# DeltaNet in a two-layer hybrid decoder: stores moved to ScalarE's and GpSimd's queues, one exponential for each head's decays, beta and the decays ahead of the first convolution

## The chip, the cores and the metric

The kernel runs on one core of a Trainium2 chip. The core has TensorE for matmuls (PE in the profile, its weight loads PEld), VectorE (DVE) and ScalarE (ACT) for elementwise work, GpSimd (POOL), and SyncE (SP), which here only issues DMAs. ScalarE and GpSimd can issue DMAs too; a DMA stands in the issuing engine's instruction queue like any other instruction. The metric is the device time of the whole program in microseconds, the median of several executions. Lower is better.

## The reference

A trunk of two layers over 16 meta tokens and 512 tokens, width 1024: retention, SwiGLU FFN, gated DeltaNet, SwiGLU FFN, and a last RMSNorm. The change lies in DeltaNet alone:

```python
qkv = jax.nn.silu(causal_conv(qkv, conv_w))            # four taps
q = l2norm(q) * (DN_DK ** -0.5); k = l2norm(k)          # 8 heads, dk 128, dv 256
beta = jax.nn.sigmoid(beta_in) * vmask
g = -jnp.exp(a_log) * jax.nn.softplus(a_in + dt_bias) * vmask
# per chunk of a head:
gam = jnp.cumsum(gc, axis=-2)
decay = jnp.exp(jnp.where(incl, gam - jnp.swapaxes(gam, -1, -2), -jnp.inf))
a_mat = jnp.where(strict, bc * kk * decay, 0.0)
sol = triangular_solve(eye + a_mat, [vc * bc, kc * bc * jnp.exp(gam)])
v_new = u - w @ state
qk = (qc @ kc.T) * decay
o = (qc * jnp.exp(gam)) @ state + qk @ v_new
state = state * jnp.exp(g_last) + (kc * jnp.exp(g_last - gam)).T @ v_new
```

Then each head's output is normed, multiplied by the Silu of its gate and projected.

## The kernel before

**Tiling.** Tokens are 16 meta tokens (NM) and 512 others in four chunks of 128; most tiles hold 128 channels by 528 tokens. Every fp32 weight tile and activation is split into a rounded part and a rest: ScalarE writes the rounded part (`whi`, L179 or L460), VectorE the rest (`wlo`, L180 or L461), and TensorE makes three matmuls for one (L470). Raw weight tiles `wraw` are fetched by SyncE (L173) into four buffers.

**Order of the work.** The program text is written out by a planner. A gemm calls `tick` once per slice of 128 contracted rows (6 matmuls of 264 columns); other work is written as Python generators that wait in a heap with a due time in ticks (`spawn`), and each `yield n` puts the next part n ticks later. The framework under it then orders each engine's instructions by their readiness in its own model, with the written order as priority, so that a late-written instruction whose inputs are ready can come before an earlier one that waits. On the chip each engine then works through its own queue in that order.

**DeltaNet** (`deltanet`, from L1764):

1. The first two q and k tiles are multiplied (`gemm_pair`) while the row norm `rb` is finished. Then `dn_gates` is spawned with no delay, so its first part is written after the first slice of the next gemm.
2. `dn_keys` runs for eight heads: a gemm for k and one for q, each followed by `conv_evac` (PSUM times `rb` into `pad` on VectorE, L1202; first tap on ScalarE, L1205; three taps on VectorE, L1207; Silu on ScalarE, L1210), a store of the tile to DRAM (`d_kq`, L1378), and its split `z` (L460, L461). Two `pad` buffers alternate. q tiles get their sums of squares in `dn_norms` (L1400). 13 ticks later comes `dn_attention`: 128x128 products, the vectors `ssk`, `cc`, `kws`, `irk`, the product of scores, `cc` and decays into `vs` (L1446), and a store of it to DRAM (`d_mp`, L1454).
3. `dn_gates` makes what the heads' decays need, in parts: first part (to L1246) 32 matmuls for beta and the decay inputs (L1235) into one large PSUM tile, one evacuation (L1243); 3 ticks later the second part (to L1289), transposes by small matmuls (L1252), sigmoid and softplus by exponentials (L1263, L1269) and a series on VectorE, up to `g` (L1281); 6 ticks later cumulative sums (L1292), their store to DRAM (`d_g`, L1305) and its broadcast load per head (`rows_in`, L1311) into `dec`; 3 ticks later the meta decays `decm0`. Then for each pair of heads GpSimd adds a triangular mask of 1e30 to `dec` (L1356), and ScalarE takes four exponentials per head, one per chunk, with scale -1 and the chunk's sums as per-row bias (L1363). `dec` uses three buffers for even pairs (tag `zh`) and three for odd ones (`zl`); the gates' own work takes one of each first. The second head of pairs 2 and 3 therefore waits until a head of pair 0 or 1 has been used. If a head's attention comes due before its decays, it drives the generator forward (L1407).
4. After the last head: `dn_inverse` loads the 32x32 diagonal blocks of `d_mp` (L1491, SyncE and ScalarE), solves them by substitution on VectorE (L1466 to L1478), stores them (L1496, L1497), and does the same for the meta tokens by way of `d_m0` and `d_m1` (L1498 to L1507). Beside it run value gemms (`dn_values`) and gate gemms (`dn_silu_gate`, with the store `d_sg`, L1608).
5. Four pairs of heads go through `dn_merge` (blocks up to 128x128; it loads `u` from `d_x`, L1515, and transposes it, L1516), `dn_scan` and `dn_gated`, between further value, gate and output gemms.

**Who issues what.** Before the change SyncE issues nearly all DMAs of this layer: weight loads, `d_kq`, `d_mp`, `d_g`, `d_m0`, `d_m1`, `d_sg` and the loads of `u`. Its queue is in order: a store that waits for its data holds up the loads behind it.

Of the kernel before, what the change touches and what calls it, by code (L numbers as in the profile page):

```python
# [10 lines left out]
AF = mybir.ActivationFunctionType  # L11
ALU = mybir.AluOpType
# [4 lines left out]
KT = D // P  # L17
NM = 16
NT = 512
T = NM + NT  # L20
HH = T // 2
# [29 lines left out]
PAIRS_APART = 14  # L51
MASKED = 4
VALUES = 6
GATE_STEPS = (3, 6, 3)
# [5 lines left out]
class Hybrid:  # L60
# [1130 lines left out]
    def conv_silu(self, w, x, rb, mt):  # L1191

        nc = self.nc
        p = self.psum_g()
        self.gemm(p, w, x, range(KT))
        return self.conv_evac(p, rb, mt)

    def conv_evac(self, p, rb, mt):
        nc = self.nc
        self.pads.reverse()  # L1200
        pad = self.pads[0]
        nc.vector.tensor_tensor(self.halves(pad[:, 3 : 3 + T]), p[:, :, :HH], self.halves(rb), op=ALU.mult)  # L1202
        acc = self.t(self.tp, [P, T], "ra", bufs=4)
# [9 lines left out]
    def dn_gates(self, sp, x, rb):  # L1213


        nc, a = self.nc, self.a
# [13 lines left out]
        nc.vector.tensor_copy(pick[32:48], self.ident[32:48, 32:48])  # L1230
        p = self.psum_g()
        for kt in range(KT):
            for i in range(2):
                for half in range(2):
                    nc.tensor.matmul(  # L1235
                        p[:48, half, :HH],
                        wst[:, kt, :],
# [4 lines left out]
        ba = self.t(self.tp, [P, T], "ra", bufs=4)[:48]  # L1242
        nc.vector.tensor_tensor(self.halves(ba), p[:48, :, :HH], self.halves(rb[:48, :]), op=ALU.mult)  # L1243
        bm = self.t(self.tp, [P, 96], "am", bufs=1)
# [101 lines left out]
        for pair in range(DH // 2):  # L1346
# [13 lines left out]
            for hd in hds:  # L1360
                for c in range(4):
                    o, de = (c + 1) * DH + hd, self.dec[hd][:, c]
                    nc.scalar.activation(de, de, AF.Exp, scale=-1.0, bias=sums[:, o : o + 1])  # L1363
            self.decays = 2 * pair + 2

    def dn_keys(self, pool, hd, x, rb, first, gt):

        nc, a = self.nc, self.a
        for s, base in ((1, 0), (0, 8)):
            if first is None:  # L1370
                w = self.load_w(a["w_dqk"][hd, 1 - s])
                p = self.psum_g()
                self.gemm(p, w, x, range(KT))
            else:
                p = first.pop(0)
            t_ = self.conv_evac(p, rb, base + hd)
            real = t_[:, NM:].rearrange("p (c i) -> p c i", c=4)
            nc.sync.dma_start(self.d_kq[:, hd, :, s, :], real)  # L1378
            if s == 1:
# [24 lines left out]
    def dn_attention(self, pool, hd, zh, zl, gt):  # L1404
# [40 lines left out]
        for c in range(4):  # L1445
# [7 lines left out]
            )  # L1453
        nc.sync.dma_start(self.d_mp[:, 4 * hd : 4 * hd + 4], mp)  # L1454
        nc.vector.scalar_tensor_tensor(
# [25 lines left out]
    def dn_inverse(self, sp):  # L1481
# [11 lines left out]
        for b in range(4):  # L1493
# [3 lines left out]
            eng.dma_start(self.d_mp[bs, :, 0, bs].rearrange("j q i -> q j i"), d[bs])  # L1497
        nc.sync.dma_start(self.d_m0, self.decm0)  # L1498
        nc.sync.dma_start(dm, self.d_m0.rearrange("j h i -> h j i"))
        yield from self.substitute(dm, tmp, NM)  # L1500
        nc.sync.dma_start(self.d_m1.rearrange("j h i -> h j i"), dm)
        um = self.t(sp, [96, DH, NM], "rr")
        nc.gpsimd.memset(um, 0.0)
        for b in range(3):
            (nc.sync, nc.scalar)[b % 2].dma_start(um[32 * b : 32 * b + NM], self.d_m1)
        nc.scalar.copy(self.um, um)
        nc.vector.tensor_tensor(self.um[64:96], um[64:96], self.um[64:96].bitcast(F32), op=ALU.subtract)  # L1507

    def dn_merge(self, hd, z, sp):
# [4 lines left out]
        ut = self.t(sp, [P, 4, 32], "wl")  # L1514
        nc.sync.dma_start(uc, self.d_x[:, 4 * hd : 4 * hd + 4])  # L1515
        nc.vector.transpose(ut.rearrange("p a b -> p (a b)"), uc.rearrange("p a b -> p (a b)"))  # L1516
# [81 lines left out]
    def dn_silu_gate(self, hd, x, rb):  # L1598
# [8 lines left out]
        nc.scalar.activation(sg, sg, AF.Silu)  # L1607
        nc.sync.dma_start(self.d_sg[:, hd], sg)  # L1608

# [154 lines left out]
    def deltanet(self, st, ctx, nxt):  # L1764
# [44 lines left out]
        rb = st["rb"]  # L1809
        gt = self.spawn(self.dn_gates(sp, x, rb))  # L1810
        for hd in range(DH):
# [276 lines left out]
```

## Time and profile before

| what | us |
|---|---|
| median of 3 executions | 1672.09 |
| lowest, highest of them | 1669.11, 1672.17 |
| the profiled execution's own time | 1669.76 |
| its span, first to last instruction | 1668.0 |
| its mean granted TensorE clock | 0.996 |
| the window from 795 to 942 (keys and attention of DeltaNet) | 147, TensorE busy 140.44 |
| 942 to 1000 (inverse) | 58, TensorE busy 56.56 |
| 1000 to 1325 (merges, scans, outputs) | 325, TensorE busy 320.02 |

Line numbers (L470) are those of the kernel before. A matmul's end is modelled and matmuls overlap, so busy TensorE isn't TensorE at its best rate: it helps to count matmuls per window and to look at the granted clock, too. A row of waits has the waiting instruction, who ended the wait, the total, the number of times and the longest. A group's row has line, engine, operation, output and inputs, shapes, count, then busy time and mean duration, then idle time of the engine before them. DMA issues of an engine aren't counted as busy; in timelines they stand with a q behind the engine's name, and a number ahead of a bracketed arrow is idle time and who ended it.

### The profile page before, as it was taken

Reading aid. Unit: us, or ns where it says so; the run is one execution under the profiler, and the core shown is the slowest. Engines: PE = TensorE matmul, PEld = TensorE weight load, DVE = VectorE, ACT = ScalarE, POOL = GpSimd, SP = SyncE. Lnnn points to the kernel's source line nnn. Section 1 sums busy time; section 2 is a strip of 40 time slices with the busy share of each in tenths; the row PEclk is TensorE's granted clock in tenths of the full one; section 3 lists DMA queues with packets and bytes.
Section 4 is the critical chain, followed back from the end, with each engine's and each line's share of the span. In section 5 each row is a group of like instructions: output and inputs, shape, how many; then the busy total and the mean of one; then the engine's idle time right before and its main releaser. Section 6 shows DMA issues by size and latency. Waiting matters only on the chain.

```text
span 1668.0 us, 30777 instructions
## 1 busy us (share of the span) xinstructions
PE 1643.1 (99%) x12415; PEld 1550.9 (93%) x12415; DVE 1297.6 (78%) x2121; ACT 886.1 (53%) x1536; POOL 99.7 (6%) x139
## 2 busy tenths in 40 slices
PE   9999999999999999999989999999999999999998
PEld 9999999999999999999989988888877889999896
DVE  7886877798698887784689888796876798888672
ACT  5445555555345545543595427776663455555542
POOL 1000000000000000000030000010100000000010
PEclk9999999999999999999999999999999999999999
DMA  6564746565323332453354554432323223333451
GB/s 211 175 165 119 219 111 198 176 210 167 113 89 102 102 102 82 122 155 101 102 158 159 140 143 139 156 104 89 107 75 114 90 89 113 102 107 110 114 163 52
DMA packets 91888, 214.54 MB, mean 129 GB/s; under 512 B 20394, under 2 KB 42146, under 8 KB 90466
## 3 DMA queue, kind: packets, MB, share of 16 engines
q1 hardware_dynamic: 80066, 194.21, 35.3%
q0 software_dynamic: 4688, 16.53, 5.7%
q10 hardware_dynamic: 6992, 1.85, 0.5%
q8 instruction: 97, 1.59, 0.4%
q14 instruction: 45, 0.37, 0.1%
HBM read 190.30 MB, written 22.25 MB: 127 GB/s over the span
## 4 chain that ended last, share of the span: by engine, by line
PE 86%; DVE 9%; ACT 3%; issue 2%; POOL 1%; POOLq 0%; ACTq 0%; DVEq 0%
PE g L470 66%; PE m L470 14%; DVE wlo L461 1%; ACT whi L460 1%; DVE wsum L220 1%; DVE ra L1207 1%; PE m L573 0%; DVE flt L461 0%; POOL ss L1686 0%; PE m L559 0%; PE m L704 0%; DVE wlo L180 0%; DVE wraw L312 0%; DVE flb L461 0%; PE m L143 0%
## 5 line engine op out<-in xcount | busy, mean ns | idle before, releaser
L460 ACT CAST whi<-wraw 128x1024 fp32r<-128x1024 f32 x171 | 179.2, 1051 | 192.5 <-PE g L470 69.4
L470 PE MATMUL g<-fht,whi 128*128 128x264 f32 (+1 forms) x976 | 277.4, 284 | 0.8 <-DVE h L338 0.7
L470 PE MATMUL g<-fht,wlo 128*128 128x264 f32 (+1 forms) x976 | 276.1, 283 | 0.8 <-DVE wlo L461 0.8
L470 PE MATMUL g<-flt,whi 128*128 128x264 f32 (+1 forms) x976 | 275.9, 283 | 0.0
L470 PE MATMUL g<-xlo,whi 128*128 128x264 f32 (+1 forms) x1088 | 260.9, 306 | 0.0
L470 PE MATMUL g<-xhi,whi 128*128 128x264 f32 (+1 forms) x1024 | 251.8, 310 | 4.6 <-ACT whi L179 4.0
L470 PE MATMUL g<-xhi,wlo 128*128 128x264 f32 (+1 forms) x1024 | 251.2, 308 | 2.3 <-DVE wlo L180 2.3
L461 DVE TENSOR_TENSOR wlo<-wraw,whi 128x1024 fp32r<-128x1024 f32 x171 | 210.5, 1234 | 46.5 <-ACT whi L460 46.2
L179 ACT CAST whi<-wraw 128x1024 fp32r<-128x1024 f32 (+3 forms) x117 | 118.1, 1011 | 138.5 <-PE g L470 107.1
L470 PEld LDWEIGHTS g<-fht,whi 128*128 128x128 f32 x976 | 183.8, 188 | 1.3 <-ACT ra L540 0.9
L470 PEld LDWEIGHTS g<-fht,wlo 128*128 128x128 f32 x976 | 183.6, 188 | 1.1 <-DVE wlo L461 1.0
L470 PEld LDWEIGHTS g<-flt,whi 128*128 128x128 f32 x976 | 183.7, 188 | 0.5
L470 PEld LDWEIGHTS g<-xlo,whi 128*128 128x128 f32 x1088 | 176.7, 189 | 7.0 <-DVE xlo L529 0.2
L470 PEld LDWEIGHTS g<-xhi,whi 128*128 128x128 f32 x1024 | 167.8, 190 | 12.4 <-ACT whi L179 4.2
L470 PEld LDWEIGHTS g<-xhi,wlo 128*128 128x128 f32 x1024 | 167.3, 189 | 10.1 <-DVE wlo L180 3.3
L180 DVE TENSOR_TENSOR wlo<-wraw,whi 128x1024 fp32r<-128x1024 f32 (+3 forms) x117 | 138.0, 1180 | 40.5 <-ACT whi L179 39.5
L470 PE MATMUL g<-fhb,whi 128*128 128x264 f32 (+1 forms) x480 | 137.4, 286 | 0.0
L470 PE MATMUL g<-fhb,wlo 128*128 128x264 f32 (+1 forms) x480 | 136.1, 284 | 1.0 <-DVE wlo L461 0.8
L470 PE MATMUL g<-flb,whi 128*128 128x264 f32 (+1 forms) x480 | 135.7, 283 | 0.0
L461 DVE TENSOR_TENSOR wlo<-wsum,whi 128x1024 fp32r<-128x1024 f32 x54 | 66.1, 1225 | 44.5 <-ACT whi L460 44.5
L470 PEld LDWEIGHTS g<-fhb,wlo 128*128 128x128 f32 x480 | 90.3, 188 | 1.8 <-DVE wlo L461 1.8
L470 PEld LDWEIGHTS g<-flb,whi 128*128 128x128 f32 x480 | 90.3, 188 | 0.5
(562 smaller groups left out, 3804.4 us busy)
## 6 DMA issues: line engine op xcount, KB each, us to landing
wraw<-in_w_gu_dram SPq DMA_DIRECT2D x66, 512.0 KB, 3.4
wraw<-in_w_ret_dram SPq DMA_DIRECT2D x56, 512.0 KB, 3.7
sraw<-in_w_gu_dram SPq DMA_DIRECT2D x22, 512.0 KB, 4.1
wraw<-in_w_ret_dram POOLq DMA_DIRECT2D x18, 512.0 KB, 5.6
wraw<-in_w_dqk_dram SPq DMA_DIRECT2D x16, 512.0 KB, 3.4
wraw<-in_w_dv_dram SPq DMA_DIRECT2D x16, 512.0 KB, 3.3
wraw<-in_w_dg_dram SPq DMA_DIRECT2D x16, 512.0 KB, 3.9
wraw<-in_w_do_dram SPq DMA_DIRECT2D x16, 512.0 KB, 3.4
```

The lines of the kernel that those rows point to most:

```text
L179: nc.scalar.copy(hi[:, c], raw[:, c])
L180: nc.vector.tensor_tensor(lo[:, c], raw[:, c], hi[:, c].bitcast(F32), op=ALU.subtract)
L220: nc.vector.scalar_tensor_tensor(dst[:, k, :], hh[:, kb + k, cs], g[:, kb + k : kb + k + 1], rb[:, cs], op0=ALU.mult, op1=ALU.mult)
L460: self.nc.scalar.copy(hi, src)
L461: self.nc.vector.tensor_tensor(lo, src, hi.bitcast(F32), op=ALU.subtract)
L470: mm(o, l, r[which], start=first and n == 0, stop=last and n == 2, **kw)
L1207: nc.vector.scalar_tensor_tensor(acc, pad[:, i : i + T], cw[:, mt, i : i + 1], acc, op0=ALU.mult, op1=ALU.add)
```

## The change

Four things are changed, all in DeltaNet.

- **Queues.** The stores `d_kq` (16) and `d_sg` (8) are issued by ScalarE, the stores `d_mp` (8), `d_m0`, `d_m1`, the load back of `d_m0`, the three loads of `d_m1` and the eight loads of `u` by GpSimd.
- **Exponentials.** Per head, four Identity activations (one per chunk, 128x128, the same scale and bias as before) are followed, 2 ticks later (RAISED), by one Exp over 128x512 in place.
- **Gates first.** Both first convolutions are evacuated to `pad` at once; then the first two parts of `dn_gates` are written with no tick between them, and only then the first head's taps. The third part is due 6 ticks later as before.
- **PSUM.** The first part's matmuls go to two small PSUM tiles, evacuated one by one, and no longer to one large one.

```diff
@@ -1193,13 +1194,16 @@
-        return self.conv_evac(p, rb, mt)
+        return self.conv_taps(self.conv_pad(p, rb), mt)
 
-    def conv_evac(self, p, rb, mt):
-        nc = self.nc
+    def conv_pad(self, p, rb):
         self.pads.reverse()
         pad = self.pads[0]
-        nc.vector.tensor_tensor(self.halves(pad[:, 3 : 3 + T]), p[:, :, :HH], self.halves(rb), op=ALU.mult)
+        self.nc.vector.tensor_tensor(self.halves(pad[:, 3 : 3 + T]), p[:, :, :HH], self.halves(rb), op=ALU.mult)
+        return pad
+
+    def conv_taps(self, pad, mt):
+        nc = self.nc
         acc = self.t(self.tp, [P, T], "ra", bufs=4)
...
@@ -1228,19 +1232,21 @@
-        p = self.psum_g()
+        p = [self.psum_m()[:48, :HH] for half in range(2)]
...
-                        p[:48, half, :HH],
+                        p[half],
...
-        nc.vector.tensor_tensor(self.halves(ba), p[:48, :, :HH], self.halves(rb[:48, :]), op=ALU.mult)
+        for half in range(2):
+            hs = slice(half * HH, half * HH + HH)
+            nc.vector.tensor_tensor(ba[:, hs], p[half], rb[:48, hs], op=ALU.mult)
@@ -1360,7 +1366,10 @@
-                    nc.scalar.activation(de, de, AF.Exp, scale=-1.0, bias=sums[:, o : o + 1])
+                    nc.scalar.activation(de, de, AF.Identity, scale=-1.0, bias=sums[:, o : o + 1])
+            yield RAISED
+            for hd in hds:
+                nc.scalar.activation(self.dec[hd], self.dec[hd], AF.Exp)
@@ -1369,13 +1378,11 @@
-                p = self.psum_g()
-                self.gemm(p, w, x, range(KT))
+                t_ = self.conv_silu(w, x, rb, base + hd)
             else:
-                p = first.pop(0)
-            t_ = self.conv_evac(p, rb, base + hd)
+                t_ = self.conv_taps(first.pop(0), base + hd)
...
-            nc.sync.dma_start(self.d_kq[:, hd, :, s, :], real)
+            nc.scalar.dma_start(self.d_kq[:, hd, :, s, :], real)
...
-        nc.sync.dma_start(self.d_mp[:, 4 * hd : 4 * hd + 4], mp)
+        nc.gpsimd.dma_start(self.d_mp[:, 4 * hd : 4 * hd + 4], mp)
...
-        nc.sync.dma_start(self.d_m0, self.decm0)
-        nc.sync.dma_start(dm, self.d_m0.rearrange("j h i -> h j i"))
+        nc.gpsimd.dma_start(self.d_m0, self.decm0)
+        nc.gpsimd.dma_start(dm, self.d_m0.rearrange("j h i -> h j i"))
...
-        nc.sync.dma_start(self.d_m1.rearrange("j h i -> h j i"), dm)
+        nc.gpsimd.dma_start(self.d_m1.rearrange("j h i -> h j i"), dm)
...
-            (nc.sync, nc.scalar)[b % 2].dma_start(um[32 * b : 32 * b + NM], self.d_m1)
+            nc.gpsimd.dma_start(um[32 * b : 32 * b + NM], self.d_m1)
...
-        nc.sync.dma_start(uc, self.d_x[:, 4 * hd : 4 * hd + 4])
+        nc.gpsimd.dma_start(uc, self.d_x[:, 4 * hd : 4 * hd + 4])
...
-        nc.sync.dma_start(self.d_sg[:, hd], sg)
+        nc.scalar.dma_start(self.d_sg[:, hd], sg)
...
@@ -1807,7 +1814,11 @@
         rb = st["rb"]
-        gt = self.spawn(self.dn_gates(sp, x, rb))
+        first = [self.conv_pad(p, rb) for p in first]
+        gt = self.dn_gates(sp, x, rb)
+        for _ in range(2):
+            next(gt)
+        self.spawn(gt, GATE_STEPS[1])
         for hd in range(DH):
```

More of the change, by code (lines that the diff above doesn't have):

```diff
@@ L52 @@
 MASKED = 4
+RAISED = 2
 VALUES = 6
```

## The prediction

> **What bounds the kernel now.** I read the page first: busy time, share of the span and instructions of each engine.
>
> ```profile
> PE 1643.1 (99%) x12415; PEld 1550.9 (93%) x12415; DVE 1297.6 (78%) x2121; ACT 886.1 (53%) x1536; POOL 99.7 (6%) x139
> ```
>
> TensorE sets the time, and the change takes no matmul away. It can win only where TensorE waits or is slowed, or lose by a new wait. So the second view is the table of windows over the key stage of DeltaNet (columns: window; its length; busy us of TensorE, its weight loads, VectorE, ScalarE and GpSimd with instruction counts; granted TensorE clock; DMA share; GB/s).
>
> ```profile
> 826.00:851.00 25.00, 25.00 (x219) 24.84 (x219) 21.72 (x54) 20.74 (x52) 13.22 (x10) 1.00 0.58 159
> 851.00:861.90 10.90, 9.04 (x71) 8.43 (x70) 9.27 (x26) 10.20 (x23) 0.00 (x0) 1.00 0.43 146
> 861.90:866.20 4.30, 0.31 (x4) 0.07 (x2) 4.04 (x16) 4.27 (x8) 1.16 (x1) 0.97 0.26 84
> 866.20:872.60 6.40, 5.85 (x25) 5.54 (x26) 5.51 (x8) 6.34 (x14) 0.00 (x0) 0.50 0.75 172
> 872.60:897.60 25.00, 25.00 (x209) 25.00 (x209) 20.63 (x59) 15.96 (x32) 3.63 (x3) 1.00 0.51 174
> ```
>
> The last row is the healthy rate: 209 matmuls in 25 us, 0.1196 us each. By it the 71 matmuls of the second row need 8.5 us of its 10.9 (2.4 lost), the 4 of the third 0.5 of 4.3 (3.8 lost), the 25 of the fourth 3.0 of 6.4 (3.4 lost, nearly all to the clock at 0.50). That is **9.6 us between 851 and 872.6**. The first row, 219 matmuls in 25 us, has the healthy rate, so nothing is to be won in the 25 us ahead of the hole.
>
> Who ended TensorE's waits there (table of waits, TensorE alone, 850 to 870; us in total, times, longest):
>
> ```profile
> PE g L470 <- ACT whi L179: 4.0, 1, 4.0
> PE m L1424 <- DVE km L616: 1.0, 1, 1.0
> ```
>
> The long one waits for ScalarE's rounding of a weight tile. The chain of waits of the same stretch (start, us, what) tells why ScalarE was late:
>
> ```profile
> 854.40 1.28 ACT L1363
> 855.70 0.44 ACT zh L1363 x2
> ...
> 856.41 1.28 ACT L1210
> ...
> 859.50 1.28 ACT L1363
> 860.80 1.21 ACT zh L1363 x4
> ...
> 862.10 1.28 ACT L1210
> ```
>
> The 1.28 us entries are loads of the activation table, to Exp for the decays (L1363) and back to Silu (L1210). From 854 to 863 ScalarE spends 4 x 1.28 + 0.44 + 1.21 = 6.8 us on six exponentials and the loads around them. The code writes eight in a row, but here two and four of them stand apart with Silus between: the order on an engine goes by readiness, and late-written exponentials fill gaps.
>
> **The change part by part.** *One exponential per head.* ScalarE's groups from 801 to 872.5 (busy us, mean ns | idle before):
>
> ```profile
> L1210 ACT ACT_TABLE_LOAD x8 | 10.3, 1283 | 0.1
> L179 ACT CAST whi<-wraw 128x1024 fp32r<-128x1024 f32 x9 | 9.3, 1047 | 0.0
> L1205 ACT ACTIVATE ra<-pad,convw 128x528 f32<-128x528 f32 x9 | 6.6, 729 | 2.6 <-DVE pad L1202 2.6
> L1363 ACT ACT_TABLE_LOAD x5 | 6.4, 1283 | 0.1
> L1210 ACT ACTIVATE ra<-ra 128x528 f32<-128x528 f32 x9 | 5.8, 645 | 5.1 <-DVE ra L1207 5.0
> ```
>
> The 32 exponentials become 32 Identities of the same shape and operands (0.3 us each, by the chain's 1.21 for four, so no change), and 8 exponentials of 128x512 come on top. None of that width is in this trace; the Silu of 128x528 takes 0.645, so I take 0.63, or 8 x 0.63 = 5.0 us. Identity isn't in the trace either: nothing more if it needs no table, up to 2 x 1.28 us for each time it would break into the Silus. I take nothing, since the nine Copies (L1205) stand among Silus and exponentials without one load of their own. What it removes: a head's decays can break into the Silus once, not two or three times. Of the five loads for L1363 here, each with a way back, I expect two or three to go, 2 to 3 x 2.57 = 5 to 8 us. ScalarE's sum over the stage is then about even (bounds: 5 more if no load goes, 3 less); what matters is where the loads stand.
>
> The Trainium skill, "ScalarE: Activation LUTs", section "What ACT_TABLE_LOAD costs", has about 1283 ns for a load plus a drain of about 1380 ns, 2.66 us a switch. In the chain the load at 854.40 ends at 855.68 and the exponential starts at 855.70, so no drain shows here. By the page the pairs removed would be worth 10 to 16 us; the measurement decides.
>
> *Beta and the decays first.* Their present times (timelines of the engines: start, us, engine, line, operation):
>
> ```profile
> 806.07 0.41 PE L1235 MATMUL g<-xhi,zl 128*48 128x264 f32 x2
> ...
> 822.74 0.20 DVE L1281 SCALAR_TENSOR_TENSOR g__01460_9425<-zh,alog__01448_9330 128x40 f32<-128x40 f32 x1
> ...
> 833.20 3.53 POOL L1356 TENSOR_TENSOR zh<-zh,kh 128x512 f32<-128x512 f32 x2 [5.96 <-DMA zh<-d_g]
> ```
>
> From L1235 to g takes 16.7 us, because taps of convolutions stand between and three ticks separate the first two steps. Without these the chain is 4 us of matmuls, some 2.5 us of evacuation, transposes and copies, and about 19 small VectorE steps of the 0.2 us that the L1281 row shows: near 11 us, so g comes some 5 us earlier (bounds: 0, if readiness had already decided it, and 7). The store of the sums, its broadcast loads and the additions (L1356) follow. Two evacuations of half width for one cost VectorE perhaps 0.2 us; two small PSUM banks for a big one leave a gemm bank free. The first head's taps come some 4 us later; nothing waits for them before that head's attention, thirteen ticks on. Heads 0 to 4 and 6 can then have their exponentials before 851. Heads 5 and 7 can't: their buffers come free only when heads 0 and 2 have read theirs.
>
> *Stores from ScalarE.* L1378 and L1608 issue behind the Silu that makes their data. SyncE's waits from 801 to 872.5, the store's own row, and ScalarE's timeline at the inverse:
>
> ```profile
> SPq L1378 <- ACT ra L1210: 20.5, 6, 5.2
> ```
> ```profile
> L1378 SPq DMA_DIRECT2D d_kq<-ra x16: 359/371/918, 809.1 to 923.1; - x16
> ```
> ```profile
> 941.21 1.08 ACTq L1491 DMA_DIRECT2D z<-d_mp  x2
> 942.33 0.47 ACT L1579 ACTIVATE v<-m,irk 96x256 fp32r<-96x256 f32 x1 [2.00 <-issue]
> ```
>
> SyncE stood 20.5 us behind Silus, but no wait of TensorE above names a DMA, so freeing it gains 0 here (at most part of the 0.55 us that is left of the hole after the long wait). On ScalarE a store costs its issue, 0.37 us by its row on SyncE; the last row shows ScalarE idle for 2.00 us while a DMA at its head waits. Queued behind each store are the cast of the same Silu's output (L460) and the next rounding (L179), for which TensorE waits. Bounds: 0 where ScalarE has slack, 16 x 0.37 = 5.9 us over the stage; three fall into the critical stretch, 1.1 us. The eight gate stores fall beside the scans: 0 to 3.0 us, I take 0.5.
>
> *Stores and loads from GpSimd.* The list of DMA issues (KB each, median us to landing), then VectorE's timeline where the inverse starts, SyncE's u loads and the transpose behind them:
>
> ```profile
> wraw<-in_w_ret_dram POOLq DMA_DIRECT2D x18, 512.0 KB, 5.6
> ...
> d_mp<-vs SPq DMA_DIRECT2D x8, 512.0 KB, 2.7
> ...
> fnw<-in_fnw_dram POOLq DMA_DIRECT2D x1, 512.0 KB, 4.0
> ```
> ```profile
> 947.06 0.69 DVE L1466 TENSOR_SCALAR z<-z 128x1024 f32<-128x1024 f32 x1 [0.52 <-DMA z<-d_mp]
> ```
> ```profile
> 1055.06 1.40 SPq L1515 DMA_DIRECT2D wh<-d_x  x2
> ```
> ```profile
> 1057.57 0.30 DVE L1516 STREAM_TRANSPOSE wl<-wh 128x128 f32<-128x128 f32 x1
> ```
>
> 512 KB from GpSimd's queue land in 4.0 to 5.6 us against 2.7, so 1.3 to 2.9 later. Of the d_mp stores only the last has a reader near: the inverse at 947.06 waits for it. TensorE has value and gate gemms to do there, so of 1.3 to 2.9 us I count 0.5 on the end (bounds 0 and 2.9). The u load that ends its transpose's wait in the last two rows has no slack for 1.3 us: I count 0.2 (bounds 0 and 2.9). The small meta-token loads run beside the big steps: 0, and as a rival below.
>
> **Sum.** In the critical stretch ScalarE loses 6.8 us of loads and exponentials and gains 1.1 of stores; if head 5's decays still fall here, also 2.57 + 0.63 + 4 x 0.3 = 4.4. Relief is 1.3 or 5.7 us; I take the middle, 3.5, against 3.8 lost in the gap. The 1.0 us wait for km lies in a window whose clock stayed at 1.00, so a rest of that size keeps the clock. Then 3.8 falls to 0.6 and 3.4 to 0.2; the 2.4 ahead falls to 1.4, as small gate steps leave VectorE's queue earlier. 9.6 becomes 2.2, **7.4 gained**. Back go 0.5 + 0.5 + 0.2 = 1.2. What is late next is VectorE, 21 to 22 us busy in 25. The profiled execution took 1669.76: 1669.76 - 6.2 = 1663.6. It lies 2.3 below the median of 1672.09 but inside the three runs' spread (1669.11 to 1672.17), so I say **1664**; this case alone spans 1659 to 1668.
>
> **The rivals.**
> *All of it goes* (0.08): heads 5 and 7 miss the stretch too, 9.6 gained, 1660, by the spread of the runs 1657 to 1662.
> *It doesn't do what it says* (0.16): each head's one exponential still parks between Silus, and relief is 1.3 us or nothing. For it: ScalarE's sum is even. Against it: g is earlier. 1669.
> *GpSimd's queue* (0.10): the last d_mp store, then the store and the loads of the meta inverse, each 1.3 to 2.9 later, one behind the other: 4 to 8 us at the scans' start, of which TensorE's gemms hide some. The 6.2 are given back: 1669. The Trainium skill, "SBUF — State Buffer" (the box "The 'DVE blocks DMA' trap"), has GpSimd unable to write descriptors while VectorE holds the shared port; the trace shows the later landing, not its cause.
> *Slower* (0.16): ScalarE from 845 to 866. No pair of loads goes, and four wide exponentials (2.5) and six stores (2.2) come in: the gap grows by 4.7, all of it at TensorE, since ScalarE is busy for 4.27 of the gap's 4.30. 1669.76 + 4.7 = 1674.5, from the median 1676.8: 1676. It decides once stores and wide exponentials outweigh the loads saved, that is with fewer than two pairs saved.
>
> **How the numbers follow.** The forecast has 0.50. About 0.2% (3.3 us) is what a measurement of this kernel can tell from no change. Faster: 0.50 + 0.08 = 0.58. Same: 0.16 + 0.10 = 0.26. Slower: 0.16. The range takes in the forecast, the cases at 1669 and the edges of the two others: 1657 to 1676.
>
> **What would show it.** Right: fewer than five table loads for the decays by 872, g near 817, the first additions near 828, no wait for whi over 1 us near 862, a clock of 1.00 from 850 to 875. Wrong: a wait of TensorE of 3 us or more between 845 and 880 behind loads and stores on ScalarE, or new idle time of TensorE ahead of the first merges near 1000.

## The result and the profile after

| what | before | after |
|---|---|---|
| median (lowest to highest) of five executions, us | 1670.46 (1669.11 to 1672.17) | 1686.95 (1683.33 to 1688.53) |
| the profiled execution's own time, us | 1669.76 | 1688.53 |
| its span, us, and granted clock | 1668.0, 0.996 | 1686.7, 0.990 |

The ratio is 1.0094, 95% interval 1.0080 to 1.0108: the change makes the kernel **15.7 us slower** (0.0094 x 1670.5). The prediction said 1664 and a range up to 1676; both the sign and the range were wrong.

The page after, busy time by engine:

```profile
PE 1650.7 (98%) x12415; PEld 1556.8 (92%) x12415; DVE 1295.3 (77%) x2122; ACT 885.0 (52%) x1540; POOL 112.8 (7%) x161
```

TensorE makes the same 12415 matmuls as before, so the time was lost in waits between them or at a lower clock. To place it I take, from all matmul rows of a trace, the distance from one start to the next less the pitch of that width in undisturbed stretches (0.122 us for 264 columns, 0.233 for 512, 0.117 for 256, for others columns / 2.4 ns + 6 ns). This "lost time" counts waits and a halved clock together. It is 79.0 us before and 96.6 after, 17.6 more: 3.4 more from 800 to 950, **10.9 more from 950 to 1025**, 3.2 more from 1025 to 1400, 0.1 elsewhere. Only such differences are used below. The level depends on the pitch taken for the narrowest matmuls (98.1 and 115.8 us, if the formula is used down to 1 column); the differences by stretch move by 0.1 us at most. Outside the three stretches, where the program wasn't changed, the profiled executions of the runs below differ from before by up to 2.6 us, so a difference of 1 or 2 us between two single traces says little.

The changed kernel's waits of TensorE alone, 800 to 1025 (us in total, times, longest), answer to the waits shown of before:

```profile
PE g L471 <- ACT whi L180: 13.2, 3, 8.6
PE m L1431 <- DVE km L617: 1.3, 1, 1.3
```

Before, the longest wait near 1000 was one of 1.4 us, in this row of the same table:

```profile
PE g L470 <- DVE wlo L180: 2.3, 3, 1.4
```

So one wait of 8.6 us is new (the expectations below call it 8.8, the length of its whole window). Windows of the changed kernel, the key stage first, then the place of that wait (columns as in the prediction; the DMA share is the time that DMA packets took, as a share of 16 engines' time):

```profile
826.00:851.00 25.00, 20.27 (x164) 19.60 (x163) 19.85 (x56) 19.34 (x47) 13.17 (x11) 1.00 0.55 169
851.00:876.00 25.00, 22.42 (x151) 21.81 (x151) 17.78 (x40) 21.14 (x48) 1.19 (x1) 0.80 0.40 124
...
1000.30:1009.10 8.80, 0.22 (x2) 0.01 (x1) 1.71 (x6) 2.19 (x4) 2.27 (x5) 0.78 0.64 200
1009.10:1014.00 4.90, 4.84 (x19) 4.30 (x19) 4.18 (x5) 2.76 (x6) 0.00 (x0) 0.50 0.64 209
```

From 826 to 851, where TensorE ran without a gap before, it is now idle for almost 5 us: the old hole moved 14 us ahead. From 1000.3 to 1009.1 almost nothing runs on TensorE, and for the next 9.8 us, until 1019.0, its granted clock is 0.50 (the last row shows the first half of that). ScalarE's and then GpSimd's timeline show what the long wait hangs on:

```profile
993.58 0.90 ACTq L1504 DMA_DIRECT2D d_mp<-z  x1
1006.91 0.30 ACT L1513 CAST um<-rr 96x128 fp32r<-96x128 f32 x1 [20.14 <-DMA z<-d_mp]
1007.12 1.05 ACT L1614 ACTIVATE sg<-sg 128x1024 f32<-128x1024 f32 x1
1008.07 1.03 ACT L180 CAST whi<-wraw 128x1024 fp32r<-128x1024 f32 x1
```
```profile
994.39 0.62 POOL L1508 DMA_DIRECT2D d_m<-z  x1 [47.40 <-DVE z L1485]
999.93 1.63 POOL L1512 DMA_DIRECT2D rr<-d_m  x3 [4.92 <-issue]
1001.69 1.14 POOL L1522 DMA_DIRECT2D wh<-d_x  x2
```

ScalarE does nothing for 12 us but wait to round `um`, the meta tokens' inverse, which comes in by three loads of 8 KB from GpSimd's queue (`rr`, landed at 1003.7, 1006.0 and 1006.8; the bracket names another DMA, one of several that are waited for, but the last to land ahead of 1006.91 is `rr`). Behind it in ScalarE's queue stand a Silu and the rounding of the weight tile that TensorE needs. The kernel before had the same step elsewhere (its ScalarE timeline):

```profile
997.68 0.32 ACTq L1505 DMA_DIRECT2D rr<-d_m  x1
998.16 1.99 ACT L179 CAST whi<-wraw 128x1024 fp32r<-128x1024 f32 x2
1000.71 1.23 ACT L1521 COPY oq<-wl 32x128 f32<-32x128 f32 x4 [0.56 <-DVE wl L1516]
1002.37 0.27 ACT L1534 COPY rh<-m 128x128 f32<-128x128 f32 x1 [0.44 <-PE m L1526]
1004.42 0.30 ACT L1506 CAST um<-rr 96x128 fp32r<-96x128 f32 x1 [1.78 <-DMA rr<-d_m]
```

There two weight roundings stand ahead of `um`.

### The profile page after: what moved, and what is told of

It is laid out like the page before. It is cut to its first block, busy times and chain, and to the rows that moved or that the text cites. A ratio compares the mean times of both kernels' runs of the same rounds, so it can differ in the third digit from the quotient of the medians.

```text
span 1686.7 us, 30754 instructions
## 1 busy us (share of the span) xinstructions
PE 1650.7 (98%) x12415; PEld 1556.8 (92%) x12415; DVE 1295.3 (77%) x2122; ACT 885.0 (52%) x1540; POOL 112.8 (7%) x161
## 4 chain that ended last, share of the span: by engine, by line
PE 77%; DVE 12%; ACT 3%; issue 3%; DMA 3%; POOL 1%; ACTq 0%; SPq 0%; POOLq 0%; DVEq 0%
PE g L471 59%; PE m L471 14%; DVE wlo L462 2%; DVE ra L1211 1%; DVE wlo L181 1%; ACT whi L461 1%; DVE z L1485 1%; DVE z L1479 1%; DVE wsum L221 1%; DVE wraw L313 1%; DVE vs L1453 0%; PE m L574 0%; DVE flt L462 0%; POOL ss L1693 0%; PE m L560 0%
```

## The experiments

All ratios are to the kernel before, run on the same chip beside each experiment. Lost time is in us, by the same count as above, for the stretches 800 to 950, 950 to 1025 and 1025 to 1400 of the profiled execution.

| run | median us | ratio (95%) | lost 800 | 950 | 1025 |
|---|---|---|---|---|---|
| before | 1670.5 | 1 | 16.4 | 2.6 | 31.2 |
| after | 1687.0 | 1.0094 (1.0080 to 1.0108) | 19.8 | 13.5 | 34.4 |
| 1 after, meta chain back | 1681.6 | 1.0057 (1.0040 to 1.0074) | 18.5 | 6.6 | 34.5 |
| 2 after, um's steps on GpSimd | 1691.1 | 1.0112 (1.0096 to 1.0127) | 20.0 | 13.6 | 36.5 |
| 3 before + meta chain | 1674.6 | 1.0020 (1.0010 to 1.0031) | 15.7 | 7.0 | 30.8 |
| 4 after, all of GpSimd's back | 1674.1 | 1.0013 (1.0003 to 1.0024) | 17.6 | 2.5 | 32.4 |
| 5 before + one Exp | 1668.0 | 0.9981 (0.9968 to 0.9993) | 14.0 | 2.7 | 31.8 |
| 6 before + gates first | 1670.7 | 0.9991 (0.9979 to 1.0002) | 15.4 | 2.8 | 31.6 |
| 7 before + ScalarE's stores | 1673.2 | 1.0004 (0.9992 to 1.0015) | 16.3 | 2.7 | 32.3 |
| 8 after, only d_mp on GpSimd | 1676.1 | 1.0020 (1.0008 to 1.0033) | 18.8 | 2.4 | 32.4 |
| 9 before + one Exp + gates first | 1672.4 | 1.0010 (0.9999 to 1.0022) | 17.7 | 5.5 | 30.3 |
| 10 run 9, sums subtracted by GpSimd | 1672.4 | 1.0007 (0.9997 to 1.0017) | 16.7 | 2.6 | 30.7 |
| 11 run 5, sums subtracted by GpSimd | 1670.3 | 0.9998 (0.9989 to 1.0008) | 16.3 | 2.6 | 30.0 |
| 12 after, loads of d_m1 back | 1680.0 | 1.0054 (1.0035 to 1.0073) | 18.9 | 4.4 | 33.6 |
| 13 before + u loads | 1673.3 | 1.0010 (0.9998 to 1.0022) | 15.8 | 2.9 | 34.6 |
| 14 before + all queue changes | 1685.4 | 1.0075 (1.0048 to 1.0102) | 16.4 | 11.6 | 34.5 |
| 15 before + meta chain + u | 1677.0 | 1.0047 (1.0032 to 1.0062) | 15.4 | 6.8 | 33.5 |
| 16 before + meta chain + d_mp | 1675.5 | 1.0027 (1.0016 to 1.0039) | 16.6 | 6.8 | 31.0 |
| 17 before + meta chain + d_sg | 1681.3 | 1.0061 (1.0044 to 1.0078) | 15.6 | 10.7 | 33.3 |
| 18 after, d_sg back on SyncE | 1680.8 | 1.0055 (1.0040 to 1.0070) | 17.6 | 7.7 | 33.7 |

"Before + meta chain" means that part of the change alone. The framework orders each engine's instructions anew for every program, so an edit of one queue can shift others; where an order matters below, it is that of the timeline or of the program. Waits of TensorE are those of its matmuls in the table of waits; the expectations have some of them 0.1 to 0.2 us longer. Differences in us are ratio differences times 1670.5.

**First: which of GpSimd's DMAs (runs 1 to 4).** Run 1, and run 4 with `d_mp` and `uc` in the same way:

```diff
-        nc.gpsimd.dma_start(self.d_m0, self.decm0)
-        nc.gpsimd.dma_start(dm, self.d_m0.rearrange("j h i -> h j i"))
+        nc.sync.dma_start(self.d_m0, self.decm0)
+        nc.sync.dma_start(dm, self.d_m0.rearrange("j h i -> h j i"))
...
-        nc.gpsimd.dma_start(self.d_m1.rearrange("j h i -> h j i"), dm)
+        nc.sync.dma_start(self.d_m1.rearrange("j h i -> h j i"), dm)
...
-            nc.gpsimd.dma_start(um[32 * b : 32 * b + NM], self.d_m1)
+            (nc.sync, nc.scalar)[b % 2].dma_start(um[32 * b : 32 * b + NM], self.d_m1)
```

> The changed kernel with only the meta-token chain (d_m0, its load back, d_m1, its three loads) back on SyncE and ScalarE. Theory Q (ScalarE's queue): in the changed kernel ScalarE's rounding of the meta block (um) was ordered ahead of a Silu and of the rounding of the next weight tile, and stands 20.1 us for the loads from GpSimd's queue; TensorE waits 8.8 us behind it and runs the next 5 us at clock 0.50, 10.7 us by the windows from 975 to 1025. With a load on ScalarE again the rounding is ordered behind two weight tiles: no wait of TensorE over 2 us from 990 to 1020, and 1686.95 - 10.7 = 1676 (1674 to 1679). Theory L (late d_mp store or late u loads hold the inverse; the meta chain only shows it): these two stay on GpSimd, so the wait stays at 5 us or more and the time at 1683 or above.

> The changed kernel with every DMA that went to GpSimd back on SyncE and ScalarE (d_mp, meta chain, u); ScalarE's stores, the one exponential and the order of the gates stay. Theory Q: the meta chain is nearly all of what GpSimd's queue costs, so this equals the run with the meta chain back, 1676, within 2 us. If the d_mp stores and u loads cost by themselves (my prediction had 0.7 for them, bounds 0 and 5.8), it is lower by that. What is left above 1670.5 then belongs to the other three parts.

Run 1 is 6.2 us better than after, not 10.7; run 4 is 13.5 better. So GpSimd's DMAs make nearly the whole loss (13.5 of 15.7), but the meta chain isn't all of it. In run 1 `um` is ordered behind weight tiles, as theory Q said, yet VectorE's transposes of `u` stand ahead of the rest of a weight tile, and TensorE waits 3.2 us at 1001.1.

Run 2 moves the two steps themselves, run 3 moves the chain in the kernel before:

```diff
-        nc.scalar.copy(self.um, um)
-        nc.vector.tensor_tensor(self.um[64:96], um[64:96], self.um[64:96].bitcast(F32), op=ALU.subtract)
+        nc.gpsimd.tensor_copy(self.um, um)
+        nc.gpsimd.tensor_tensor(self.um[64:96], um[64:96], self.um[64:96].bitcast(F32), op=ALU.subtract)
```

> The changed kernel with all its DMAs as they are, and only the two small steps on um (rounding and rest) moved from ScalarE and VectorE to GpSimd. Theory Q: it is the place in ScalarE's queue that costs, not the landing; the loads land as late as before (about 6 us after their issue), but no weight rounding stands behind them: the 8.8 us wait goes and the time is near 1676 (1674 to 1680). Rival (the landing itself): the matmuls that read um are due just then, TensorE then waits 5 us or more for um, and the time stays above 1682.

> The kernel before with only the meta-token chain moved to GpSimd's queue. Theory Q: the order on ScalarE flips in the same way (um ahead of a Silu and a weight rounding), so a wait of TensorE of 7 to 10 us appears near 1000 with half clock behind it: 1670.5 + 8 to 11 = 1679 to 1681. Theory L: without the d_mp store and the u loads on GpSimd the chain is not late: under 2 us, 1670 to 1673.

Theory Q missed in both. In run 2 the rival's numbers came (over 1682, a wait over 5 us), but not by its mechanism: TensorE doesn't wait for `um` itself. The wait only changed its engine (waits of VectorE from 998 to 1012):

```profile
DVE u L617 <- POOL um L1514: 11.3, 1, 11.3
DVE wl L1523 <- DMA wh<-d_x: 1.6, 2, 1.4
```

VectorE's cast of `um` (L617) is ordered ahead of a weight's rest, and TensorE waited 10.5 us for that rest. In run 3 `um` stands ahead of a Silu and a weight rounding exactly as after the change, but TensorE waited only 3.2 us. So the place in the queue opens the hole, and something else sets its size: the `d_m1` loads landed 1.9 us after their issue in run 3 and 5.6 after the change.

**The other parts alone (runs 5 to 8).**

> The kernel before with only the exponentials changed (four Identities and one Exp of 128x512 per head). The three parts left when GpSimd's DMAs are taken back (one Exp, ScalarE's stores, gates first) cost 2.5 us together. Theory P (place in ScalarE's queue): 8 Exps of 0.63 us come in (5.0), four loads of 1.28 go (5.1), so ScalarE's sum is even, and the hole near 862 stays with 3 to 4.5 us of waiting for whi: 1670 to 1673. My prediction's step (relief by table loads that go): the hole falls under 1.5 us and the time to 1664 to 1667.

> The kernel before with only beta and the decays ahead of the first convolution (and the two small PSUM tiles). Theory P: the exponentials are ready sooner, and the hole at TensorE moves some 12 us ahead, from 862 to 850, with its size (8 to 11 us in all from 825 to 875): 1669 to 1673. My prediction's step: g 5 us earlier lets heads 0 to 4 and 6 be done before 851, loss under 5 us, time 1665 to 1668.

> The kernel before with only the d_kq and d_sg stores on ScalarE. My prediction has 1.1 us in the key stage and 0.5 beside the scans: 1672 to 1674. Rival (SyncE was the bound: it stood 20.5 us behind Silus, and loads behind them come sooner): 1667 to 1670. Third (ScalarE's stores cost nothing): 1670.5 to 1672.

> The changed kernel with the meta chain and the u loads back on SyncE and ScalarE, and only the eight d_mp stores left on GpSimd. With everything of GpSimd's back it took 1674.1, with the meta chain alone back 1681.6: 7.5 us belong to the d_mp stores or to the u loads. Theory U (the u loads: the transpose that waits for them stands on VectorE ahead of the rests of two weight tiles, as um did on ScalarE): 1674 to 1676. Theory M (the d_mp stores land later and hold the inverse): 1679 to 1682, with TensorE's loss at 1000 as in that run (about 6 us).

One Exp alone gains 3.2 us (interval 1.2 to 5.3), of which the lost time shows 2.4 in the key stage; the longest wait there is 2.9 us, and for VectorE, instead of 4.0 for ScalarE. Theory P's 1670 to 1673 missed it, and the 1664 to 1667 by my prediction's step missed the median of 1668.0 by 1 us. Gates first alone moves the hole ahead and gains 1.5 (-0.3 to 3.5), ScalarE's stores alone cost 0.7 (-1.3 to 2.5): no change lies inside both. The `d_mp` stores on GpSimd cost 1.2 (runs 8 and 4, 1.0020 against 1.0013; runs 16 and 3 have the same difference), which the intervals don't tell from nothing; theory U was right. So in the changed kernel the `u` loads make 6.2 us of run 1's excess over run 8.

**Together (runs 9 to 11).** Run 9 is the change without any queue; runs 10 and 11 take the 32 Identities off ScalarE:

```diff
+                sc = sums[:, DH + hd : 5 * DH : DH].unsqueeze(2).to_broadcast([P, 4, P])
+                nc.gpsimd.tensor_tensor(self.dec[hd], self.dec[hd], sc, op=ALU.subtract)
                 nc.gpsimd.tensor_tensor(
...
-                for c in range(4):
-                    o, de = (c + 1) * DH + hd, self.dec[hd][:, c]
-                    nc.scalar.activation(de, de, AF.Identity, scale=-1.0, bias=sums[:, o : o + 1])
-            yield RAISED
-            for hd in hds:
-                nc.scalar.activation(self.dec[hd], self.dec[hd], AF.Exp)
+                nc.scalar.activation(self.dec[hd], self.dec[hd], AF.Exp, scale=-1.0)
```

> The kernel before with one exponential per head and the gates first, all queues as before. Alone they gave -3.2 and -1.5 us, ScalarE's stores +0.7, and all three together +2.2 to 2.5, so 6 us are lost when they meet. Theory S (the stores meet the other two on ScalarE in the key stage): without the stores the two add up, 1666 to 1667.5. Theory G (exponential and early gates lose when together, since both put ScalarE's work into the same stretch from 830 to 850): 1670.5 to 1673 already without the stores.

> As the run before it (one exponential, gates first, queues as before), but the sums are subtracted by GpSimd in a second 128x512 step, and the 32 Identities on ScalarE (0.3 us each, 9.6 us) are gone; Exp takes scale -1. Theory P (ScalarE's place in the key stage is the bound): 1.2 us per head less in front of the weight roundings; the hole of 4 us near 848 falls under 2.5 and the time is 2 to 4 us under that run, 1663 to 1667. Rival (GpSimd's additions, 1.3 us per head more, come too late, and the exponentials stand in ScalarE's queue for them): not faster, 1669 or more, with waits of ScalarE for GpSimd over 4 us.

> The kernel before with the subtraction on GpSimd and one exponential per head; gates and queues as before. Theory P: better than one Exp with Identities (1668.0) by what 32 activations weigh in the stretch: 1664 to 1667. Rival as in the run before: 1669 or more.

Theory G was right about the time: alone -3.2 and -1.5, together +1.7 (-0.2 to 3.7) already without the stores. Run 9's waits of TensorE from 845 to 856, then two rows of its VectorE timeline:

```profile
PE g L471 <- DVE pad L1202: 3.6, 1, 3.6
PE g L471 <- ACT whi L180: 1.0, 1, 1.0
```
```profile
848.52 1.66 DVE L1453 SCALAR_TENSOR_TENSOR vs<-m,cc,zh 128x256 f32<-128x256 f32 x4
...
853.97 0.69 DVE L1202 TENSOR_TENSOR pad<-g,rb 128x528 f32<-128x528 f32 x1
```

With whi's wait down to 1.0 us TensorE waits 3.6 for VectorE, whose evacuation (L1202) stands at the end of 5.5 us without a gap: products of scores with the decays that are now there early, taps, a split. So where theory G had ScalarE's work in mind, it is VectorE's that ends the long wait; that the early decays cause it is read from the order, and no run tests it. The prediction had named VectorE as late next, but left only 2.2 us of the whole hole. Run 9's profiled execution also lost 2.9 more than before from 950 to 1025: its granted clock was 0.50 from 1014.4 to 1021.2 (shown in the last section). This execution took 1675.6, above the median of 1672.4, so the 2.9 may be its own. Taking the Identities away brought nothing: ScalarE waited for GpSimd's two steps instead, 5.9 + 4.8 us in run 10 (4.1 + 3.2 in run 9, from 800 to 900), and TensorE's one long wait there, 6.4 us, is again for VectorE. The rival was right in both runs; run 5 stays the best version, 0.9981 of before.

**Place or landing (runs 12 to 14).** Run 12 takes only the three loads of `d_m1` back; runs 13 and 14 make queue changes alone.

> The changed kernel with only the three loads of d_m1 back on SyncE and ScalarE; d_m0, d_m1's store, d_mp and u stay on GpSimd. In the program ScalarE's rounding of um now stands behind one Silu, one weight rounding and most copies of u; on VectorE the transposes of u and one rest of a weight stand ahead of it. Theory Q (place in the queue): the wait at 1000 falls from 8.8 to what the u loads hold, 3 to 5 us: 1680 to 1683. Rival (the landing: GpSimd's loads land 6 us after their issue and SyncE's 3.7): the wait falls by 2 to 3 us and the time is 1684 or above.

> The kernel before with only the eight u loads on GpSimd. In the program the first of the two transposes that read them now stands on VectorE ahead of the rest of a weight tile (wlo) that TensorE is due to read. Theory Q (place in the queue): the wait for wlo near 997 grows from 1.6 to 3 us or more, the clock falls to 0.50 for some 5 us behind it, and the time is 1674 to 1677. Rival (u loads cost only when they queue on GpSimd behind the loads of um, which wait for d_m1): 1670 to 1672.5, wait near 997 under 2 us.

> The kernel before with all queue changes (ScalarE's and GpSimd's) and neither the one exponential nor the gates first. Theory Q (the order that the queues bring costs by itself): um stands ahead of a Silu and a weight rounding on ScalarE and the transposes ahead of a wlo on VectorE, as in the changed kernel, so 10 to 14 us: 1681 to 1686, with one wait of 7 to 10 us near 998. Rival (it needs the shift by the other parts): 1674 to 1678, wait under 5 us.

Run 12: the wait at 1001 fell from 8.6 to 1.4 us, more than either theory said, and the time by 6.7. Run 13: the wait near 997 was 1.6, the rival's value, but 3.4 us more were lost beside the scans (1025 to 1400), and the time is 1.7 up with no change just inside the interval. Run 14: the queues alone bring 12.5 us and one wait of 8.9 us at 998.0, so the loss needs neither the exponentials nor the gates. The singles (0.7 + 3.3 + 1.7 + 1.2 = 6.9) don't add up to 12.5. The intervals alone would allow that, but none of the singles has a wait over 3.2 us near 1000, and run 14 has 8.9: some of the moves make each other worse.

**Which two (runs 15 to 18).** Run 15 adds the `u` loads to the meta chain, run 16 the `d_mp` stores:

> The kernel before with the meta chain and the u loads on GpSimd, the d_mp stores on SyncE. Alone they gave +3.0 (meta) and +2.4 (u). Theory A (the u loads behind them on the queue make the loads of um land late): median landing of the d_m1 loads 4 us or more, one wait of TensorE of 7 to 10 us near 998, 1681 to 1686. Theory B (the d_mp stores or ScalarE's stores do it): landing under 3 us, wait 3 to 4 us, 1675 to 1677.

> The kernel before with the meta chain and the d_mp stores on GpSimd, the u loads on SyncE. Theory A: the d_m1 loads land in under 3 us as with the meta chain alone, wait 3 to 4 us, 1674 to 1677. Theory B: landing 4 us or more, wait 7 to 10 us, 1680 to 1685.

Neither does it: landings of 1.8 and 1.9 us, waits of 3.5 and 3.1. Run 15 rules out theory A, run 16 the `d_mp` half of theory B; ScalarE's stores are left. What runs 3, 15 and 16 share is SyncE. Run 3's waits of SyncE from 985 to 1002:

```profile
SPq L1608 <- ACT sg L1607: 5.2, 1, 5.2
```

SyncE stands at a gate store, whose Silu is queued on ScalarE behind `um`. So while `um`'s loads fly (995.4 to 998.3) hardly anything else does: run 3's window has a DMA share of 0.08. Its window, its wait of TensorE, and the row of its DMA issues (KB each, median us to landing):

```profile
995.00:1000.00 5.00, 2.43 (x20) 2.22 (x19) 1.17 (x4) 1.63 (x3) 1.50 (x3) 0.98 0.08 22
```
```profile
PE g L470 <- ACT whi L179: 3.2, 1, 3.2
```
```profile
rr<-d_m POOLq DMA_DIRECT2D x3, 8.0 KB, 1.9
```

Run 17 adds to run 3 only the gate stores on ScalarE, and run 18 takes only these back from the changed kernel:

```diff
-        nc.sync.dma_start(self.d_sg[:, hd], sg)
+        nc.scalar.dma_start(self.d_sg[:, hd], sg)
```

> The kernel before with the meta chain on GpSimd (alone +3.0 to 3.3 us, wait 3.3) and the gate stores d_sg on ScalarE; d_kq, d_mp and u stay on SyncE. Theory F (a freed SyncE issues its 512 KB loads while the small loads of um fly): median landing of the d_m1 loads 4 us or more, one wait of TensorE of 6 to 10 us near 998 behind the rounding of um, 1679 to 1685. Rival (the wait grows with the number of DMAs on GpSimd, not with SyncE's loads): landing about 2 us, wait 3 to 4 us, 1673 to 1676.

> The changed kernel with only the gate stores d_sg back on SyncE. Theory F: SyncE stands behind the Silu again while the loads of um fly, these land in about 2 us, the wait falls from 8.8 to 3 to 4 us and the time to 1679 to 1682. Rival: no change in the wait, 1685 to 1688.

The same views of run 17, with SyncE's timeline:

```profile
995.00:1000.00 5.00, 1.48 (x13) 1.27 (x11) 0.71 (x1) 0.00 (x0) 1.51 (x3) 1.00 0.94 290
```
```profile
PE g L470 <- ACT whi L179: 8.1, 1, 8.1
```
```profile
994.77 0.36 SPq L1695 DMA_DIRECT2D sg<-d_sg  x1
995.44 0.37 SPq L1721 DMA_DIRECT2D z<-d_mp  x1
995.90 0.46 SPq L1720 DMA_DIRECT2D z<-d_kq  x1
996.41 0.50 SPq L1721 DMA_DIRECT2D z<-d_mp  x1
```
```profile
rr<-d_m POOLq DMA_DIRECT2D x3, 8.0 KB, 5.7
```

SyncE, free of the store, issues a load of 512 KB at 994.77 and three more at the moment when GpSimd issues its three of 8 KB (995.48 to 996.50). The DMA share is 0.94 instead of 0.08, the small loads land 5.7 us after their issue instead of 1.9, and the wait behind `um` is 8.1 us instead of 3.2. Of these 4.9 us more, 3.9 are the landing (the last load lands at 1002.2 instead of 998.3); 1.0 is that TensorE runs out of work at 996.5 instead of 997.4.

The meta chain alone cost 3.3, ScalarE's stores all together 0.7 and at most 2.5 (the gate stores alone were not run); the meta chain and the gate stores together cost 10.2. By the count of lost time 8.1 of it lie from 950 to 1025 (4.4 in run 3) and 2.1 beside the scans, where the cause was not followed. Run 18 is the reverse: landing 1.9 again, 6.5 us gained. Theory F's time and landing were right, but the wait fell only to 5.1, not to 3 to 4, since the loads were issued from 999.2 on, 0.3 us before TensorE ran out of work at 999.6 (in run 3 from 995.4 on, 2.0 us before).

## Why the prediction was wrong

**The step that failed** is "The small meta-token loads run beside the big steps: 0", together with the term of the gate stores, "0 to 3.0 us, I take 0.5", which priced only their issue on ScalarE. The prediction did think of a freed SyncE ("freeing it gains 0 here"), but in the key stage alone, and as a gain. By run 17 these two terms are not 0.5 together but 10.2. A second step failed as well, the relief of the hole in the key stage; it stands under "Gates first" below. The rival on GpSimd's queue named the right place (the scans' start) and the right chain; it priced the landing only (4 to 8 us, partly hidden, 1669). It missed two things. The reader of the loads, `um`'s rounding, had an engine's queue behind it, and its place there went with the DMAs: ahead of a weight rounding instead of behind two. And a store taken off SyncE lets SyncE go on: what it issues next shares the DMA engines with the small loads.

**The Trainium skill's rule** beside that rival ("SBUF — State Buffer", the box "The 'DVE blocks DMA' trap": GpSimd can't write descriptors while VectorE holds the shared port) doesn't explain the late landing here. GpSimd's three issues take the same time in runs 3 and 17 (1.50 and 1.51 us), and in run 17 VectorE does nothing from 997.2 until the last of the loads has landed at 1002.2; what differs from run 3 is the DMA share.

**GpSimd's stores and `u` loads.** For `d_mp` I expected a landing 1.3 to 2.9 us later and 0.5 us on the end. It landed 0.9 later (3.6 against 2.7 us); the rows from which I took 1.3 to 2.9 were of loads, not stores. The cost of 1.2 lies within the bounds, but the runs don't tell it from nothing and don't show the mechanism. The `u` loads were put at 0.2 and cost 1.7 alone (run 13, -0.3 to 3.7), 4.5 beside the meta chain (runs 15 and 3), 6.2 in the changed kernel; landing 2.5 against 1.9 us. Of run 13's 3.4 us beside the scans, 2.2 are waits of TensorE for two of ScalarE's steps: `vs` (L1687) 2.4 instead of 1.2, `rh` (L460) 2.2 instead of 1.2. Why these come later was not followed.

**One Exp** was right in its parts: 128x512 takes 0.61 to 0.64 us (predicted 0.63), Identity needs no table load (none stands at L1369), and in run 5 four of the 17 loads from 795 to 942 are gone, as in the changed kernel. But fewer loads aren't the step's alone, nor relief by themselves: run 14, without the one Exp, has 13 too and gains nothing in the key stage. ScalarE's groups of the changed kernel from 801 to 872.5 (8 and 5 loads before):

```profile
L1214 ACT ACT_TABLE_LOAD x5 | 6.4, 1283 | 0.1
...
L1372 ACT ACT_TABLE_LOAD x3 | 3.8, 1283 | 0.1
```

**Gates first** brought the decays forward as planned: the cumulative sums start at 818.3 (822.99 before), the additions at 829.4 (828 predicted). The error is in "nothing is to be won in the 25 us ahead of the hole": there was something to lose. ScalarE and VectorE were busy there for 20.74 and 21.72 of 25 us, and with the decays' work moved in the hole came there: run 6 by itself has a wait of 4.1 us at 850 and no long one near 862. The changed kernel's ScalarE near 848, and its waits from 826 to 870:

```profile
846.62 0.99 ACT L1369 ACTIVATE zl<-zl,kl 128x128 f32<-128x128 f32 x3
847.62 1.28 ACT L1372 ACT_TABLE_LOAD   x1
848.92 1.15 ACT L1372 ACTIVATE zl<-zl 128x512 f32<-128x512 f32 x2
849.97 1.34 ACT L1209 ACTIVATE ra<-pad,convw 128x528 f32<-128x528 f32 x2
851.22 1.03 ACT L180 CAST whi<-wraw 128x1024 fp32r<-128x1024 f32 x1
```
```profile
PE g L471 <- ACT whi L180: 4.5, 2, 3.8
```

TensorE waits 3.8 us for the last row of the timeline. So the relief of 7.4 us failed because the hole moved and did not close: one Exp and the gates together (run 9) are at +1.7 (-0.2 to 3.7).

**ScalarE's stores** were put at 1.6 us and cost 0.7 alone (-1.3 to 2.5), which holds both 1.6 and nothing; what the freed SyncE did comes on top.

**The sum.** Queues 12.5 (run 14) and the other two 1.7 (run 9) make 14.2 of the 15.7; the rest lies inside the intervals. Against the forecast of -6.2 that is 21.9 us: 11.3 from the queues (12.5 instead of 1.2) and 9.1 from the hole (+1.7 instead of -7.4, which has 1.1 us of stores in it). The prediction's own sum has a slip of 0.3: its relief of 3.5 leaves 0.3 of the 3.8 us, not the 0.6 that it writes. The signs that I named as wrong both came: over 3 us of waiting on ScalarE between 845 and 880, and new idle time of TensorE near 1000.

## What to carry to other kernels

When a DMA moves to another queue, look at three things, not one: its own landing; the step that waits for it, with what stands behind that step on its engine; and what the queue that it left will now issue, and beside which small transfers. A window in which an engine is nearly full, though TensorE has no gap there, is no place to move work to. Parts that look independent should be tried alone and in pairs: here one pair (meta chain and gate stores) cost 10.2 us where the meta chain and all of ScalarE's stores cost 4.0 by themselves, and another (one Exp and gates first) didn't gain what its parts gained.

## What the runs showed of the hardware

*Small loads beside large ones.* Three loads of 8 KB from GpSimd's queue landed after 1.8 to 1.9 us (median) where the DMA share was 0.08 to 0.15 (runs 3 and 15) and after 5.7 at a share of 0.94 (run 17). The queue by itself isn't slow: from SyncE, beside its own 512 KB loads, they took 3.6 us before and 4.4 in run 1, and the one from ScalarE took 6.4 in run 1.

*The clock.* In run 8 a wait of TensorE of 1.4 us left the granted clock at 1.00. In run 1 one of 3.2 us halved it, from 1003.3 to 1010.2, and 4.2 us more were lost from 950 to 1025 than in run 8, for 1.8 us more of waiting. Windows of run 8, then of run 1:

```profile
1000.00:1005.00 5.00, 3.55 (x29) 3.27 (x27) 2.36 (x5) 2.06 (x6) 0.00 (x0) 1.00 0.81 225
1005.00:1010.00 5.00, 5.00 (x61) 4.74 (x61) 4.67 (x9) 3.80 (x7) 0.00 (x0) 1.00 1.04 381
```
```profile
1000.00:1005.00 5.00, 1.82 (x13) 1.61 (x12) 2.56 (x5) 2.08 (x6) 0.00 (x0) 0.83 0.82 235
1005.00:1010.00 5.00, 5.00 (x33) 4.76 (x32) 2.55 (x3) 0.78 (x1) 0.00 (x0) 0.50 0.62 214
```

In both the transposes of `u` start near 1002 (1002.6 and 1001.9); the wait is 1.4 us where the weight's rest stands ahead of them on VectorE and 3.2 where they stand ahead of it.

The length of a wait doesn't decide alone. In run 11 the clock was 0.50 for 3.4 us after a wait of 2.1 us (at 849) and stayed at 1.00 after one of 3.0 us (at 860). In run 9 it was 0.50 for 6.8 us though TensorE had no wait over 0.6 us from 1003 to 1014:

```profile
1007.50:1014.40 6.90, 6.37 (x109) 5.62 (x107) 3.62 (x8) 3.49 (x11) 0.00 (x0) 1.00 0.90 328
1014.40:1021.20 6.80, 6.80 (x38) 6.44 (x39) 2.89 (x9) 4.32 (x10) 0.00 (x0) 0.50 0.35 141
```

From 800 us on, every stretch at 0.50 in these traces lasts 3.4 us or a multiple of it (3.4, 6.8, 10.2, 13.7, 17.1), but for the last, which the kernel's end cuts off. The Trainium skill, "TensorE: Matmul & The Clock Gate", section "What's actually happening", has the clock fall after an idle window of about 3.4 us, with windows that run freely. The lengths agree with such a window; the falls after waits of 3.1 us (run 16), 2.1 us (run 11) and none to speak of (run 9) don't agree with a whole idle window.

Open are why the framework put `um` earlier once its chain was on GpSimd (only the order itself is seen), what makes the clock fall where no wait is long, why ScalarE's steps beside the scans come later with the `u` loads on GpSimd, and what the gate stores on ScalarE cost alone.
